# Two decoder layers on one core: gated loads of w_down, sums on VectorE, and four smaller moves in the order of work

## The chip, the core and the metric

The kernel runs on one core of a Trainium2 chip. The metric is the device time of one execution in microseconds (us), lower is better. It is given as the median of several runs. The profile comes from one more execution, whose own time is given beside its span.

The core has a matrix engine (TensorE, PE in the profile; PEld is its loading of weights), a vector engine (VectorE, DVE), a scalar engine (ScalarE, ACT), GpSimd (POOL), and SyncE (SP), which here only starts DMA transfers. Each engine works through its own queue in order; semaphores tie the queues together. Matmul results go to PSUM, everything else of the work lies in SBUF.

## The reference

Input and output are 512 tokens of 1024 channels in float32. Two layers of this form run one after the other, and an RMS norm closes:

```python
h = rmsnorm(x, norm_mix)
proj = h @ w_in                       # q, k, v of FoX, forget logits, q and kv of NSA, gates
log_f = log_sigmoid(f_a + b_forget)
y_a = fox_attention(q_a, k_a, v_a, log_f) @ w_o_fox    # scores carry c_i - c_j, c = cumsum(log_f)
y_b = nsa_attention(q_b, kv_b, g_b) @ w_o_nsa          # compressed, selected and window branch
x = x + (sigmoid(gate_a) * y_a + sigmoid(gate_b) * y_b) @ w_out
h = rmsnorm(x, norm_mlp)
x = x + square(relu(h @ w_up)) @ w_down                # w_up 1024 x 4096, w_down 4096 x 1024
```

Both attentions have 8 heads of 64. The forget logits need log_sigmoid and a running sum over the tokens.

## The kernel before

**Precision.** float32 operands are split into a rounded part h ("hi") and a rest ("lo"): ACT casts h, and VectorE (in a few places POOL) subtracts it to get the rest. A product is three matmuls, hi·hi, hi·lo and lo·hi, which is why pairs of a cast and a subtraction appear everywhere (L217/L218 for weights, L1255/L1256 for w_down's operands, L1618/L1619 for the activations).

**Stages of a layer.** Token projections of the values and of a group g2 (NSA values, forget logits, branch gates) come first. Then, in this order in the code: the casts of g2's values into VN together with the logits z and the tanh of the gates (L883 to L892), the gates, and forget() (L785 to L810), a chain of about twenty small VectorE operations with one Exp on ACT, whose result L801 feeds the matmuls L807/L808 into PSUM bank "S" (the running sum). Then fox_proj(0), the 8 FoX heads with other projections as filling, and the NSA heads in 4 pairs with more filling. A pair ends in after() (L962 on): ACT copies one half of PSUM to a tile "tmp" (L972), VectorE adds the other half (L973), twice, and out_pair (L497/L498) makes hi and lo. Both halves of a pair share one "tmp" tile.

Once all four pairs are there, half(1, m) for m = 0 to 7 multiplies them with w_o_nsa (gemm, L243 to L245; four k-tiles, one per pair, three matmuls each), gates the result and adds it to the FoX part. mix() splits it again, and w_out follows.

**mlp().** w_up's 32 columns of 128 activations: 8 are plain, the other 24 are made in units g = 4 to 15 by a Strassen–Winograd scheme of 2 × 2 blocks, with seven products instead of eight. w_down's last columns are units g = 16 to 19 of the same scheme. Unit g has two weight rows r1 = (a11, a12) and r2 = (s1, a22), and a third tile s3. SP loads them (L1456, L1466), and sums that the scheme needs are made by DMAs that POOL issues and that add while they write ("accumulating"):

- L1458: s1 in r2's first half; L1467: s3 from s3 and a11
- L1259: a11 becomes a11 + s1 (this is s2), once a11 itself has been cast
- L1261: a12 becomes a12 + s2 (this is s4)

operands(n) (L1244) casts the next n operands of w_down in the order of plan() and issues L1259 or L1261 behind the cast concerned. The products of w_down are L1302. Its moving operands are the activations as they are ("o", "ohl") and combinations of them: combine(p) (L1264) makes for each of the four groups p a tile "tf" with three VectorE operations (L1269, and L1271 twice) out of c[p], the two activations of one w_up unit, then its hi by ACT (L1273) and lo by VectorE (L1274) into a tile "tt". The results are added into x by VectorE (L1318 to L1336).

load(g) (L1438) takes the tiles of unit g out of pools and issues its loads. For g = 18 the tiles are one "vn" tile for r2 and r1, and half a "q2" tile for s3; g = 19 takes two more "q2" tiles and the other half. A load can start as soon as its tile's last user is done.

act() (L1607) finishes a w_up output: relu and square on ACT (L1616, L1617), hi on ACT (L1618), lo on POOL (L1619). 32 such activations are made; the last ones, which unit g = 15 makes, go to tiles "ohl".

**Order.** The work is written as generators that are advanced by hand. The order on each engine then follows from a scheduler; POOL's queue holds both its own arithmetic and the accumulating DMAs, and SP's queue holds all loads, those of the next layer behind those of w_down.

Of the kernel before, what the change touches and what calls it, by code (L numbers as in the profile page):

```python
# [11 lines left out]
F32 = mybir.dt.float32  # L12
F32R = mybir.dt.float32r
AF = mybir.ActivationFunctionType
OP = mybir.AluOpType
# [4 lines left out]
T = 512  # L20
KT = D // 128
NB = T // 128
# [10 lines left out]
OFF, N_SMALL = {}, 0  # L33
# [104 lines left out]
def run(*gens):  # L138
    for g in gens:
        for _ in g:  # L140
            pass


class Body:
# [471 lines left out]
    def compress(self, kc, vc, small, l):  # L616
# [20 lines left out]
        def load(c):  # L637
            for i, raw in enumerate(self.two("o2", "w1", F32) if c < 8 else ()):
                nc.sync.dma_start(raw, a["w1"][l, i, c].rearrange("p j m -> p (j m)"))
                loaded.append(raw)  # L640

        load(0)
        load(1)
        for c in range(0, 8, 2):
            load(c + 2)
# [205 lines left out]
    def layer(self, l, u):  # L851
        nc, a = self.nc, self.a
# [10 lines left out]
        R, rc = self.rstd(self.acc, ("O", "O"), wait=g, R=self.R)  # L863
        self.rc, self.late = rc, l > 0
        run(g)
        small = self.small
        g2 = [self.p(t) for t in ("mm", "mm", "O", "O")]
        g = self.token_proj([[a["wg2"][l, c].rearrange("p j m -> p (j m)")] for c in range(4)], 288, g2, u)
        VF = []
        for b in range(NB):  # L870
# [4 lines left out]
                                           op0=OP.mult, op1=OP.subtract)  # L875
# [2 lines left out]
        VN = self.t("vn", [128, NB, 4, 128], F32R)  # L878
        z = self.t("z", [128, NB, 8])
        th = self.t("th", [128, NB, 24])  # L880
        rch = self.t("s4", [128, NB], name="rch")
        nc.vector.tensor_scalar(rch, rc, 0.5, None, op0=OP.mult)
        for b in range(NB):  # L883
            pv = g2[b][:, :256].rearrange("p (h d) -> p h d", h=4)
            r = rc[:, b:b + 1]
            nc.vector.scalar_tensor_tensor(z[:, b], g2[b][:, 256:264], r, small[:, OFF["bf"]:OFF["bf"] + 8],
                                           op0=OP.mult, op1=OP.add)
            nc.scalar.activation(th[:, b], g2[b][:, 264:288], AF.Tanh, scale=rch[:, b:b + 1])
            nc.scalar.activation(VN[:, b, :, :64], pv, AF.Copy, scale=r)
            nc.vector.scalar_tensor_tensor(VN[:, b, :, 64:], pv, r, VN[:, b, :, :64].bitcast(F32),  # L890
                                           op0=OP.mult, op1=OP.subtract)
# [6 lines left out]
        nc.sync.dma_start(self.CRS, a["rope"])  # L898
        for i in range(2):
            nc.gpsimd.tensor_tensor(self.CRS[:, i], self.CRS[:, i], R, op=OP.mult)  # L900
        self.forget(z.rearrange("p b h -> p (b h)"))

        st, hl = {}, []

# [52 lines left out]
        def nsa_pair(p):  # L957

            hk = p // 2
            O = [None]  # L960

            def after(O):  # L962
                for e in range(2):
                    for bank in range(2):
                        nc.tensor.matmul(O[:, bank, e], self.vz[:, hk, e],
                                         self.pc[hk][p % 2][:, bank * 256:(bank + 1) * 256], start=False, stop=e == 1)
                o = self.t("zz", [128, T], name="o")
                t = self.t("tmp", [128, T])
                half = lambda x: x.rearrange("p (b c) -> p b c", b=2)
                for e in range(2):  # L970
                    s, f = slice(64 * e, 64 * e + 64), slice(64 * (1 - e), 64 * (1 - e) + 64)
                    nc.scalar.copy(half(t[s]), O[f, :, e])  # L972
                    nc.vector.tensor_add(half(o[s]), O[s, :, e], half(t[s]))  # L973
                st["ob", p] = self.out_pair(o)

            ready = (lambda: ("qb", p) in st and "ks" in st and "kw" in st, lambda: hk in self.pc)

            def unit(br, e):
                return dict(br=br, e=e, p=p, hk=hk, O=O, after=after, ready=ready[br], kk=lambda: KK[hk],
                            q=lambda: st["qb", p][:, e], v=lambda b: VN[:, b, 2 * br + hk],  # L980
                            gate=lambda: gt[:, :, 1 + br, 2 * p + e],
                            steps=(self.pair_scores, self.pair_transposes, self.pair_values))
            u = [unit(br, e) for br in range(2) for e in range(2)]
            for i in range(4):
                u[i]["other"], u[i]["second"] = u[(i + 2) % 4], u[i | 1]
            return u

        def half(kind, m, w):

            xs = ya if kind == 0 else yb  # L990
            ps = self.p("mm")
            yield from self.gemm(ps, w, 4 * (m % 2), xs, ks=4)
            st["y"] = ps
# [32 lines left out]
        yb = [st["ob", p] for p in range(4)]  # L1026
# [4 lines left out]
        def mix():  # L1031
            y = MA[len(mixed) // 2][:, len(mixed) % 2]
            h, lo = self.two("o2", "o")
            nc.scalar.activation(h, y, AF.Copy, scale=0.5)
            nc.vector.scalar_tensor_tensor(lo, y, 0.5, h.bitcast(F32), op0=OP.mult, op1=OP.subtract)
            mixed.append((h, lo))

        for m in range(8):
            if m % 2 == 0:
                w = self.weights(a["wo"][l, 1, m // 2].rearrange("p i c -> p (i c)"))  # L1040
            run(half(1, m, w))
            t, y = st["gb", m], MA[m // 2][:, m % 2]
            nc.vector.scalar_tensor_tensor(t, t, 1.0, st["y"], op0=OP.add, op1=OP.mult)
            nc.vector.tensor_add(y, y, t)
            if m % 2:
                mix()
# [9 lines left out]
        for m in range(8):  # L1056
            ps = self.bank()
            w = self.weights(a["wout"][l, m].rearrange("p k c -> p (k c)"))
# [11 lines left out]
    def mlp(self, l, x, u, acc, gm):  # L1070
# [35 lines left out]
        for j in range(self.PLAIN):  # L1106
            ps = self.bank()
            w = self.weights(a["wup"][l, j].rearrange("p k c -> p (k c)"))
            run(self.gemm(ps, w, 0, u))
            if R is None and j == 0:  # L1110
                pend.append(ps)
                continue
            if R is None:
                R, _ = self.rstd(acc, (self.turn_tag(), self.turn_tag()))
                prep = S.prepare(R)
                for p in pend:
                    act(p)
            act(ps)
            for _ in range(3):
                next(prep, None)  # L1120
# [89 lines left out]
class Strassen:  # L1210
# [33 lines left out]
    def operands(self, n):  # L1244

        b, nc = self.b, self.nc
        plan = self.plan()
        for k, g in plan[self.made:self.made + n]:
            self.made += 1
            r1, r2, s3 = self.raw[g]  # L1250

            a11, a12, s1 = r1[:, :512], r1[:, 512:], r2[:, :512]
            src = dict(a11=a11, a12=a12, s2=a11, s4=a12, s1=s1, a22=r2[:, 512:], s3=s3)
            h, lo = b.two("u2", "d")
            nc.scalar.copy(h, src[k])  # L1255
            nc.vector.tensor_tensor(lo, src[k], h.bitcast(F32), op=OP.subtract)  # L1256
            self.ops[k, g] = h, lo
            if k == "a11":
                nc.gpsimd.dma_start(a11, s1, accum_op=OP.add)  # L1259
            if k == "s2":  # L1260
                nc.gpsimd.dma_start(a12, a11, accum_op=OP.add)  # L1261
            yield
# [175 lines left out]
    def load(self, g, third=True):  # L1438

        b = self.b  # L1440
        if g == 18:
            r = b.t("vn", [128, 2, 1024], name="raw")
            r2, r1 = r[:, 0], r[:, 1]
            self.both = b.t("q2", [128, 2, 512], name="raw")
            s3 = self.both[:, 0]
        elif g == 19:
            r2, r1 = (b.t("q2", [128, 1024], name="raw") for _ in range(2))
            s3 = self.both[:, 1]
        elif g % 2:
            r2, r1, s3 = (b.t("va", [128, 1024], name="raw") for _ in range(3))  # L1450
        else:
            r2, r1 = (b.t("e", [128, 1536], name="raw") for _ in range(2))
            s3 = r1[:, 1024:]
        r1, r2, s3 = self.raw[g] = r1[:, :1024], r2[:, :1024], s3[:, :512]
        for i, t in enumerate((r2, r1)):
            self.nc.sync.dma_start(t, self.source(g, i))  # L1456
            if t is r2:
                self.nc.gpsimd.dma_start(r2[:, :512], r2[:, 512:], accum_op=OP.add)  # L1458
        if third:
            self.third(g)  # L1460
# [146 lines left out]
    def act(self, c, acts, tag):  # L1607

        b, nc = self.b, self.nc
        if tag == "kd":  # L1610
            if len(acts) % 2 == 0:
                self.late = b.t("kd" if len(acts) == 30 else "a4", [128, 4, T], F32R, name="ohl")
            h, lo = (self.late[:, len(acts) % 2 * 2 + i] for i in range(2))
        else:
            h, lo = b.two(tag, "o")
        nc.scalar.activation(c, c, AF.Relu)  # L1616
        nc.scalar.activation(c, c, AF.Square)  # L1617
        nc.scalar.copy(h, c)  # L1618
        nc.gpsimd.tensor_tensor(lo, c, h.bitcast(F32), op=OP.subtract)  # L1619
        acts.append((h, lo))  # L1620


# [34 lines left out]
```

## Time and profile before

| what | value |
|---|---|
| median of 3 runs | 1542.08 us (1542.0 to 1542.48) |
| the profiled execution's own time | 1543.98 us |
| its span | 1541.9 us |
| mean granted TensorE clock | 0.994 |
| PE, PEld busy | 1506.9 us, 1274.8 us |
| DVE, ACT, POOL busy | 1149.8 us, 835.3 us, 214.0 us |
| DMA | 199.35 MB, mean 129 GB/s |

A group or a piece of a timeline is read as: start, duration, engine, line, operation, output <- input, shape, count. In square brackets stands how long the engine was idle before it, and what ended that. A row of waits gives the engine, its tile and line, what it waited for, the total in us, the number of times and the longest. The granted clock is the share of full speed that the chip let TensorE have. A row of a table by stretches gives the stretch, its length, the busy time of each engine with the number of instructions, the granted clock, the DMA share and GB/s.

### The profile page before, as it was taken

What the parts mean: (1) busy time and instruction counts of PE and PEld (TensorE: products, weight loads), DVE (VectorE), ACT (ScalarE), POOL (GpSimd) and SP (SyncE); (2) the same over time, 40 slices, a digit from 0 to 9 for tenths busy, and PEclk for the clock granted to TensorE, in tenths of its full rate; (3) what the DMA queues carried; (4) which work ended last, traced back from release to release, by engine and by line L of the source; (5) the groups of instructions that cost most, each with busy time, mean ns of one, the idle gap of its engine ahead of it and who ended that gap; (6) DMA issues with size and microseconds to landing.
All of it is one profiled execution on the core that took longest, in us unless ns stands there. A gap on an engine that the chain in (4) does not pass through costs nothing. (4 is left out here: it accounts for less than half of the span.)

```text
span 1541.9 us, 22037 instructions
## 1 busy us (share of the span) xinstructions
PE 1506.9 (98%) x7952; PEld 1274.8 (83%) x7952; DVE 1149.8 (75%) x2188; ACT 835.3 (54%) x1580; POOL 214.0 (14%) x222
## 2 busy tenths in 40 slices
PE   9999999999999999998999999999999999999987
PEld 8888888887888888887987788888788888888976
DVE  5678978767487877787746799787674968777865
ACT  6465655554463655555534556555544637555645
POOL 4010000001200222223220000000011002212233
PEclk9999999999999999999999999999999999999999
DMA  7555422137324555556266552222453245555361
GB/s 267 158 162 134 131 69 82 56 110 211 96 96 144 144 144 138 136 138 177 75 192 169 161 136 82 93 69 69 150 171 107 91 144 144 137 140 148 96 145 61
DMA packets 73340, 199.35 MB, mean 129 GB/s; under 512 B 9200, under 2 KB 10608, under 8 KB 73232
## 3 DMA queue, kind: packets, MB, share of 16 engines
q1 hardware_dynamic: 57824, 170.41, 35.9%
q0 software_dynamic: 11520, 20.98, 7.8%
q10 hardware_dynamic: 3888, 6.58, 1.2%
q8 instruction: 62, 1.02, 0.3%
q14 instruction: 46, 0.38, 0.1%
HBM read 149.62 MB, written 4.19 MB: 100 GB/s over the span
## 5 line engine op out<-in xcount | busy, mean ns | idle before, releaser
L217 ACT CAST wh<-raw 128x1024 fp32r<-128x1024 f32 (+2 forms) x177 | 181.8, 1027 | 236.8 <-PE ps_mm L244 69.8
L218 DVE TENSOR_TENSOR wl<-raw,wh 128x1024 fp32r<-128x1024 f32 (+2 forms) x177 | 212.4, 1200 | 41.3 <-ACT wh L217 40.8
L243 PE MATMUL ps_mm<-u,wh 128*128 128x512 f32 x512 | 204.9, 400 | 0.0
L245 PE MATMUL ps_mm<-u,wl 128*128 128x512 f32 x512 | 202.0, 394 | 0.0
L244 PE MATMUL ps_mm<-u,wh 128*128 128x512 f32 x512 | 201.7, 394 | 0.0
L1486 DVE TENSOR_TENSOR s<-raw,s 128x512 fp32r<-128x512 f32 x168 | 138.4, 836 | 54.6 <-ACT s L1485 53.6
L1458 POOL DMA_DIRECT2D raw<-raw x32 | 29.1, 910 | 746.5 <-DVE wl L218 268.0
L1485 ACT CAST s<-raw 128x512 fp32r<-128x512 f32 x168 | 102.6, 620 | 29.3 <-PE ps_PT L1507 5.0
L243 PE MATMUL ps_mm<-o,wh 128*128 128x512 f32 x284 | 112.2, 396 | 1.8 <-ACT o L497 1.8
L243 PEld LDWEIGHTS ps_mm<-u,wh 128*128 128x128 f32 x512 | 96.7, 189 | 19.2 <-DVE E L457 0.8
L245 PEld LDWEIGHTS ps_mm<-u,wl 128*128 128x128 f32 x512 | 96.2, 188 | 19.7
L245 PE MATMUL ps_mm<-o,wl 128*128 128x512 f32 x284 | 111.4, 392 | 0.0
L244 PE MATMUL ps_mm<-o,wh 128*128 128x512 f32 x284 | 111.2, 392 | 0.0
L244 PEld LDWEIGHTS ps_mm<-u,wh 128*128 128x128 f32 x512 | 96.4, 188 | 16.6
L585 ACT CAST pth<-ps_PT 128x384 fp32r<-128x384 f32 (+1 forms) x96 | 49.0, 513 | 66.0 <-PE ps_PT L581 65.8
L543 DVE CUSTOM_DVE_ANT_0 E<-ps_S,ct 128x384 f32<-128x384 f32 (+3 forms) x112 | 57.3, 514 | 31.2 <-PE ps_S L556 30.3
L544 ACT ACTIVATE E<-E,tiny 128x384 f32<-128x384 f32 (+3 forms) x112 | 65.6, 586 | 20.2 <-DVE tiny L543 19.8
L243 PE MATMUL ps_PT<-o,wh 128*128 128x512 f32 x156 | 62.5, 401 | 6.0 <-DVE z L1555 6.0
L586 DVE TENSOR_TENSOR ptl<-ps_PT,pth 128x384 fp32r<-128x384 f32 (+1 forms) x96 | 56.8, 599 | 13.7 <-ACT pth L585 12.3
L243 PEld LDWEIGHTS ps_mm<-o,wh 128*128 128x128 f32 x284 | 53.3, 188 | 13.1 <-ACT o L497 2.6
L245 PEld LDWEIGHTS ps_mm<-o,wl 128*128 128x128 f32 x284 | 53.4, 188 | 11.7
L244 PEld LDWEIGHTS ps_mm<-o,wh 128*128 128x128 f32 x284 | 53.4, 188 | 10.6 <-DVE o L498 0.9
(448 smaller groups left out, 3741.4 us busy)
## 6 DMA issues: line engine op xcount, KB each, us to landing
raw<-wb SPq DMA_DIRECT2D x64, 512.0 KB
raw<-wup SPq DMA_DIRECT2D x64, 512.0 KB
raw<-wd SPq DMA_DIRECT2D x48, 512.0 KB
raw<-raw POOLq DMA_DIRECT2D x80, 256.0 KB, 4.4
w<-w SPq DMA_DIRECT2D x32, 256.0 KB
kda<-hla SPq DMA_DIRECT2D x32, 256.0 KB
q2a<-hla SPq DMA_DIRECT2D x64, 128.0 KB
raw<-wo SPq DMA_DIRECT2D x16, 512.0 KB
```

The lines of the kernel that those rows point to most:

```text
L217: nc.scalar.copy(h[:, :n], raw[:, :n])
L218: nc.vector.tensor_tensor(lo[:, :n], raw[:, :n], h[:, :n].bitcast(F32), op=OP.subtract)
L243: mm(ps, h[:, c], xh, start=start and i == 0, stop=False)
L244: mm(ps, h[:, c], xl, start=False, stop=False)
L245: mm(ps, lo[:, c], xh, start=False, stop=stop and i == ks - 1)
L543: nc.vector.tensor_tensor_reduce(e, ps, self.mask[:, T - n:], -1.0, BIG, OP.add, OP.min, mx)
L544: nc.scalar.activation(e, e, AF.Exp, bias=mx, scale=-1.0, accum_out=un["sm"][:, i:i + 1])
L585: nc.scalar.copy(h[:, e, :n], ps[:, :n])
L586: nc.vector.tensor_sub(lo[:, e, :n], ps[:, :n], h[:, e, :n].bitcast(F32))
L1458: self.nc.gpsimd.dma_start(r2[:, :512], r2[:, 512:], accum_op=OP.add)
L1485: nc.scalar.copy(h, src)
L1486: nc.vector.tensor_tensor(lo, src, h.bitcast(F32), op=OP.subtract)
```

## The change

There are six edits (line numbers of before):

1. The logits z and forget() are issued ahead of the casts of VN and the tanh of the gates (L878 to L901).
2. In a pair's after(), each half takes its own "tmp" tile (L968).
3. The last pair of heads is taken late: m = 0 and m = 1 of half(1, m) run over k-tiles 0 to 2 first, m = 0 into bank "mm" and m = 1 into bank "S", and then both take k-tile 3 (L1038 on).
4. a11 + s1 is made by VectorE, in the step that casts s2, and no longer by POOL's accumulating DMA L1259.
5. load(18) takes all tiles of units 18 and 19 at once and has ACT copy one column of c[3], which unit 15 of w_up makes last, into each of the four. The loads of units 18 and 19 write these tiles and so wait for the copies. In the queue r1 of a unit now stands ahead of r2.
6. act() has the lo half of the last two activations, 30 and 31, subtracted by VectorE, no longer by POOL.

```diff
@@ token projections, L878 @@
+        for b in range(NB):
+            nc.vector.scalar_tensor_tensor(z[:, b], g2[b][:, 256:264], rc[:, b:b + 1], small[:, OFF["bf"]:OFF["bf"] + 8],
+                                           op0=OP.mult, op1=OP.add)
+        self.forget(z.rearrange("p b h -> p (b h)"))
         rch = self.t("s4", [128, NB], name="rch")
...
-            nc.vector.scalar_tensor_tensor(z[:, b], g2[b][:, 256:264], r, small[:, OFF["bf"]:OFF["bf"] + 8],
-                                           op0=OP.mult, op1=OP.add)
...
-        self.forget(z.rearrange("p b h -> p (b h)"))
@@ after() of a pair, L965 @@
-                t = self.t("tmp", [128, T])
...
                     s, f = slice(64 * e, 64 * e + 64), slice(64 * (1 - e), 64 * (1 - e) + 64)
+                    t = self.t("tmp", [128, T])
@@ w_o_nsa, L1038 @@
-            run(half(1, m, w))
+            if m == 0:
+
+                first = [self.p(tag) for tag in ("mm", "S")]
+                for k, ks in ((0, 3), (3, 1)):
+                    for i, ps in enumerate(first):
+                        run(self.gemm(ps, w, 4 * i + k, yb[k:], ks=ks, start=k == 0, stop=k == 3))
+            if m < 2:
+                st["y"] = first[m]
+            else:
+                run(half(1, m, w))
@@ operands(), L1251 @@
+            if k == "s2":
+                nc.vector.tensor_tensor(a11, s1, a11, op=OP.add)
             h, lo = b.two("u2", "d")
             nc.scalar.copy(h, src[k])
             nc.vector.tensor_tensor(lo, src[k], h.bitcast(F32), op=OP.subtract)
             self.ops[k, g] = h, lo
-            if k == "a11":
-                nc.gpsimd.dma_start(a11, s1, accum_op=OP.add)
             if k == "s2":
                 nc.gpsimd.dma_start(a12, a11, accum_op=OP.add)
@@ load(), L1440 @@
         if g == 18:
             r = b.t("vn", [128, 2, 1024], name="raw")
+            self.rest = [b.t("q2", [128, 2, 512], name="raw") for _ in range(3)]
+
+            for t in [r] + self.rest:
+                self.nc.scalar.copy(t[:, :, :1], self.c[3][:, :, :1])
             r2, r1 = r[:, 0], r[:, 1]
-            self.both = b.t("q2", [128, 2, 512], name="raw")
-            s3 = self.both[:, 0]
+            s3 = self.rest[0][:, 0]
         elif g == 19:
-            r2, r1 = (b.t("q2", [128, 1024], name="raw") for _ in range(2))
-            s3 = self.both[:, 1]
+            r2, r1 = (t.rearrange("p a c -> p (a c)") for t in self.rest[1:])
+            s3 = self.rest[0][:, 1]
@@ act(), L1619 @@
-        nc.gpsimd.tensor_tensor(lo, c, h.bitcast(F32), op=OP.subtract)
+        (nc.vector if len(acts) > 29 else nc.gpsimd).tensor_tensor(lo, c, h.bitcast(F32), op=OP.subtract)
```

## The prediction, on record before the changed kernel ran

> **What bounds the kernel now.** First the page: is there an engine that is never idle?
>
> ```profile
> span 1541.9 us, 22037 instructions
> PE 1506.9 (98%) x7952; PEld 1274.8 (83%) x7952; DVE 1149.8 (75%) x2188; ACT 835.3 (54%) x1580; POOL 214.0 (14%) x222
> ```
>
> TensorE (PE) is. An edit can only pay where it closes a hole in PE's row, lets PE run at a higher clock, or shortens the few microseconds at both ends. No edit here removes a matmul. So the second view is the list of PE's waits, by what ended them (the columns behind the names: total, times, longest, in us).
>
> ```profile
> PE ps_PT L243 <- DVE z L1555: 6.0, 1, 6.0
> PE ps_mm L243 <- ACT o L497: 1.8, 2, 0.9
> PE ps_S L808 <- issue: 1.6, 1, 1.6
> PE ps_S L1302 <- DVE x L1328: 1.5, 1, 1.5
> ...
> PE ps_PT L1302 <- DVE x L1318: 1.5, 1, 1.5
> PE ps_PT L1302 <- ACT tt L1273: 1.4, 1, 1.4
> ...
> PE ps_PT L1302 <- POOL ohl L1619: 1.2, 1, 1.2
> ...
> PE ps_PT L1302 <- ACT ohl L1618: 1.1, 1, 1.1
> PE ps_S L808 <- DVE tiny L801: 1.0, 1, 1.0
> ...
> PE ps_mm L1302 <- POOL ohl L1619: 0.9, 1, 0.9
> ...
> PE ps_PT L1302 <- DVE tt L1274: 0.6, 1, 0.6
> ...
> PE ps_O L1302 <- DVE x L1318: 0.4, 1, 0.4
> ```
>
> Each row belongs to one place: 6.0 and L1328's 1.5 to w_down of layer 1, the seven others of L1302 (7.1 in all) to w_down of layer 0, 1.8 to the last pair of heads (one wait in each layer), L808's 1.6 and 1.0 to forget() of layers 0 and 1.
>
> Third, what ended the 6.0. ACT's, POOL's and SP's rows around it, then line 1259 (landing least, median, longest):
>
> ```profile
> 1467.06 0.62 ACT L1255 CAST d<-raw 128x512 fp32r<-128x512 f32 x1
> 1475.19 0.62 ACT L1255 CAST d<-raw 128x512 fp32r<-128x512 f32 x1 [7.50 <-DMA raw<-raw]
> ```
> ```profile
> 1468.32 1.14 POOL L1259 DMA_DIRECT2D raw<-raw  x1
> ```
> ```profile
> 1470.68 9.61 SPq L1456 DMA_DIRECT2D raw<-wdn  x3
> ```
> ```profile
> DMA to landing us min/median/max: 3.3/3.7/7.9
> ```
>
> ACT's cast of s2 needs the sum that line 1259 has a DMA make. That DMA was issued at 1468.32 and released ACT at 1475.19: 6.9 us, against a median of 3.7, while SP's loads of w_down ran over it. VectorE's queue stood behind ACT, and PE behind VectorE. Layer 0 shows the same (the 7.9).
>
> Fourth, the clock and the traffic there (span, then PE, PEld, DVE, ACT, POOL busy, granted clock, DMA share, GB/s):
>
> ```profile
> 715.00:727.00 12.00, 7.20 (x50) 6.04 (x48) 11.29 (x15) 8.88 (x14) 7.50 (x7) 1.00 0.95 232
> 727.00:730.00 3.00, 2.70 (x12) 2.70 (x13) 3.00 (x7) 0.00 (x0) 0.00 (x0) 0.50 0.18 71
> ...
> 734.00:737.00 3.00, 3.00 (x15) 3.00 (x15) 2.53 (x5) 1.66 (x3) 0.00 (x0) 0.50 0.00 0
> ...
> 1470.00:1477.00 7.00, 1.03 (x9) 0.82 (x8) 1.15 (x3) 1.81 (x4) 0.88 (x1) 0.82 1.05 297
> 1477.00:1480.00 3.00, 3.00 (x7) 2.40 (x8) 2.25 (x3) 2.97 (x6) 1.89 (x3) 0.50 0.60 128
> 1480.00:1483.00 3.00, 3.00 (x12) 2.35 (x11) 2.23 (x3) 1.17 (x3) 2.83 (x4) 0.78 0.69 143
> ```
>
> In layer 1, 0.82, 0.50 and 0.78 make 2.5 + 3.0 + 1.3 = 6.8 us at half clock; 2.5 lie before 1477, in the hole, so 4.3 us of work lose half: 2.1 us. A piece of half clock seems to last 3.4 us, and layer 0 has one about 727 and one about 734.
>
> **The change part by part.** The order of the changed kernel's instructions on each engine is known from its build; I walk through it with durations of before.
>
> *Layer 0, w_down: sums on VectorE (edit 4), lo halves on VectorE (edit 6), loads late (edit 5).*
>
> ```profile
> 715.66 0.69 DVE L1256 TENSOR_TENSOR d<-raw,d 128x512 fp32r<-128x512 f32 x1 [7.62 <-ACT d L1255]
> ...
> 720.56 1.75 DVE L1269 TENSOR_TENSOR tf<-z 128x512 f32<-128x512 f32 x1
> ```
> ```profile
> 733.68 0.74 PE L1302 MATMUL ps_PT<-tt,d 128*128 128x256 f32 x2 [0.64 <-DVE tt L1274]
> ```
>
> The sum needs no DMA any more, so VectorE's 7.62 us of idleness go. Two lo subtractions come in at 0.69 each, less about 1.1 where an operation lay beside POOL's subtraction (1.75 for what takes 0.69 alone). That is 7.3; the walk through the queue gives 7.0: the lo half of the fourth operand tile, which PE took at 733.68, is ready at 726.65. PE itself would be there at about 723.8 (733.68 less the 7.1 of waits, less 7 × 0.16 that a wait costs beside its own length, worked out at the last pair, and less 1.7 of half clock), so it waits anew, some 2.9 us. The gain is set by VectorE's chain: 7.0, plus 1.7 for the half-clock piece after 734 (the one at 727 lies ahead of that wait and costs nothing), less 1.0 for the chance that the new wait brings a piece of its own (0.6 of 1.7), less 0.2 for the new wait's own 0.16: **7.5**. From below 4.6 (two sums, 2 × 0.69, the gate copies, 0.8, and the rest of a half-clock piece, 0.7, all land on the chain), from above 9.9 (no wait left: 7.1 + 1.1 + 1.7).
>
> *Layer 1, w_down.* The 6.0 and the 2.1 of half clock go for the same reason: without them PE would reach the fourth operand tile, which it took at 1494.14, at about 1486.1. But edit 5 puts a wait in that place. The loads of pair 18 wait for gate copies behind the last cast of the activations on ACT; and VectorE's sum of pair 18 stands in its queue **ahead of** the last half of the tile's differences (L1271) and of the tile's lo half. Behind it queue those and every later addition into x; PE waits for them.
>
> ```profile
> 1480.58 0.62 ACT L1618 CAST ohl<-z 128x512 fp32r<-128x512 f32 x1
> ...
> 1492.95 1.05 ACT L1273 CAST tt<-tf 128x1024 fp32r<-128x1024 f32 x1 [1.84 <-DVE tf L1271]
> ```
> ```profile
> 1492.04 0.88 DVE L1271 SCALAR_TENSOR_TENSOR tf<-tf,z 128x256 f32<-128x256 f32 x2
> ```
> ```profile
> 1494.14 0.30 PE L1302 MATMUL ps_mm<-tt,d 128*128 128x256 f32 x1
> ```
> ```profile
> raw<-wdn SPq DMA_DIRECT2D x16, 512.0 KB
> ```
> ```profile
> DMA to landing us min/median/max: 3.3/4.7/11.2
> ```
> ```profile
> DMA to landing us min/median/max: 3.3/3.7/6.7
> ```
>
> (The last two are lines 1458 and 1467, the accumulations that make s1 and s3.) The cast that ended at 1481.2 ends some 5.8 earlier, 1475.4. The gates follow, and SP issues at 1475.7. At the 297 GB/s above, 512 KB take 1.76 us and 256 KB 0.88; the least landing, 3.3 for 256 KB, leaves 2.4 ahead of the data. So r1 is there at 1479.9, r2 at 1481.6, s3's load at 1482.5. With the medians s1 is summed at 1486.3 and s3 at 1486.2. Then 0.69 sum, 0.44 difference, 1.05 cast: the hi half is ready at 1488.5, PE waits about 2.5, and it stands where before stood at 1494.14: 5.5 gained. Then L1328's 1.5 goes: its chain of waits led to a DMA sum too, which VectorE now makes:
>
> ```profile
> 1496.66 4.46 DMA raw<-raw
> ```
>
> Less 0.6 for a chance of one in three that the new wait costs a piece of half clock: **6.4**. The ends: at the least landing (s3 then last, 1485.8) 6.9, with no half clock 7.5; at the longest (1492.8) the tile is ready at 1495.0, and the 5.5 turns into a loss of 0.9.
>
> *Last pair (edits 2, 3), both layers.*
>
> ```profile
> 352.06 0.58 ACT L972 COPY tmp<-ps_O 64x512 f32<-64x512 f32 x1 [0.75 <-DVE o L973]
> ```
> ```profile
> 352.58 0.39 PE L244 MATMUL ps_mm<-o,wh 128*128 128x512 f32 x1
> 352.81 0.39 PE L245 MATMUL ps_mm<-o,wl 128*128 128x512 f32 x1
> ```
>
> Matmuls start 0.23 apart. Five more of them, of m=1, now stand ahead of the first that needs the last pair: 1.16 us of cover against waits of 0.9. With its own tmp per half, ACT's second copy needn't wait the 0.75. Both waits go, and with each 0.16 more, because a matmul lasts 0.39 by its row and the next starts after 0.23 where nothing stops it: **2.1**. If the pair came later instead, the second PSUM bank would be the cause; ends 0 and 2.1. Elsewhere the split delays one pair by some 0.8 us, for which nobody waits.
>
> *forget() (edit 1).*
>
> ```profile
> 814.57 0.19 DVE L801 SCALAR_TENSOR_TENSOR tiny<-tiny 128x32 f32<-128x32 f32 x1
> ```
>
> L801 comes some 0.95 earlier, but its matmuls also stand five matmuls (1.16) earlier on PE, so the wait stays: **−0.3** for both layers, ends −2.3 and +1.9.
>
> *At nothing:* four gate copies per layer (0.2 each, ACT is busy 54%; they lie behind the last cast, counted above); the next layer's weights, which stand behind the gated loads on SP and are used only after this stage; if they ran late, each us would cost the next layer one.
>
> Sum: 7.5 + 6.4 + 2.1 − 0.3 = 15.7. The profiled execution took 1543.98, 2.1 more than its span and 1.9 more than the median, 1542.08. So 1528.3 on the former, **1526.4** on the latter.
>
> **The rivals.**
>
> *A. The gated loads give layer 1 back* (0.17). For it: VectorE's sum stands ahead of the tile, and landings of 11.2 occur. Against: few other loads are then under way. At 11.2 layer 1 loses 0.9 rather than gains 6.4: 1542.1 − 7.5 − 2.1 + 0.3 + 0.9 = 1533.7; so 1529.5 to 1534.
>
> *B. No new wait* (0.12). The pair lands while PE is still on older tiles, and the lists of VectorE drain faster than I walk: 9.9 + 6.1 + 2.1 + 1.7 + 2.1 − 0.3 = 21.6 gained: 1520.5; 1519.5 to 1523.
>
> *C. The new waits without half clock* (0.17). The row 727 to 730 has 0.50 although no single wait ahead of it is above 1.5 us; that bears out that short waits in a row suffice, and I have charged 1.6 for it. If they don't: 1524.8. The Trainium skill, “TensorE: Matmul & The Clock Gate”, section “HAM oscillation — how this bites in real kernels”, asks only that no idle gap exceed about 3.4 us; by that rule the new waits, each shorter, would be free, and the outcome is C. This trace speaks against the rule as far as its row at 727 goes.
>
> *D. Slower* (0.06). The same place as A, further: if s1 of pair 18 lands past 1501.2, the tile comes 9.3 us later than in before and eats the rest (7.5 + 2.1 − 0.3); at 1505.1 the time is 1546. It would need 23.5 us from issue to landing, twice the longest here.
>
> *E. Within 0.2%* (0.06): VectorE, at 11.29 of 12 us busy in layer 0, doesn't get its extra sums done (8 × 0.69) and loses there what layer 1 gains: some 1541.
>
> **How the numbers follow.** The forecast has 0.42 (1524.5 to 1529.5). The range of 8 in 10 takes in C, A and the upper half of B: 1521.5 to 1534. A measurement of this kernel tells about 0.2%, 3.1 us, from no change. Faster by more: 0.42 + 0.17 + 0.12 + 0.17 = 0.88; within: 0.06; slower: 0.06.
>
> **What would show it.** PE's waits on L1555, L497, L1318 and POOL's lo are gone; a wait on tt of 2 to 3 us stands in each w_down; VectorE's sum of pair 18 in layer 1 waits for a DMA until about 1486; L808's waits remain. Wrong if the holes of before stay, if that sum waits beyond 1490, or if PE's clock falls for more than one piece per layer.

## The result, and the profile after

The changed kernel takes 1523.56 us (median of 4 runs, 1521.22 to 1525.26), before 1542.04 (4 runs, 1541.21 to 1542.48). The ratio is 0.988, 95% interval 0.9863 to 0.9897: 18.5 us faster. The forecast was 1526.4, in a range of 1521.5 to 1534, and a gain of 15.7 us. The profiled execution took 1524.42, 19.6 less than that of before.

The head of the page, and the rows of PE's waits that answer to those of before (the line numbers have moved: L1302 is now L1312, tt's L1273 and L1274 are L1283 and L1284):

```profile
span 1522.6 us, 22041 instructions
...
PE 1500.2 (99%) x7952; PEld 1271.8 (84%) x7952; DVE 1147.7 (75%) x2200; ACT 836.0 (55%) x1588; POOL 201.5 (13%) x210
```
```profile
PE ps_mm L1312 <- ACT tt L1283: 2.8, 1, 2.8
PE ps_PT L1312 <- ACT tt L1283: 1.6, 1, 1.6
...
PE ps_S L808 <- DVE tiny L801: 0.8, 1, 0.8
...
PE ps_PT L1312 <- DVE tt L1284: 0.6, 1, 0.6
...
PE ps_S L808 <- issue: 0.4, 1, 0.4
```

The 6.0 behind VectorE's z, the 1.8 of the last pairs, POOL's lo halves, and the waits on x L1318, L1324 and L1328 are gone. What stands in w_down now, up to the last stage of layer 1, are waits for the fourth operand tile tt: 1.6 and 0.6 in layer 0, 2.8 in layer 1.

Both traces have 7952 matmuls, so the start of the n-th in each (counted from 0) tells how far ahead the changed kernel is, and the step between two such points what a stage gave:

| matmul n | before | after | ahead | step | stage between |
|---|---|---|---|---|---|
| 200 | 38.97 | 38.55 | 0.4 | 0.4 | start of the program |
| 1000 | 191.38 | 189.84 | 1.5 | 1.1 | forget() of layer 0 |
| 1600 | 308.68 | 306.92 | 1.8 | 0.2 | |
| 2000 | 393.52 | 390.41 | 3.1 | 1.3 | last pair, layer 0 |
| 3500 | 694.53 | 691.55 | 3.0 | −0.1 | |
| 3950 | 764.57 | 753.25 | 11.3 | 8.3 | w_down, layer 0 |
| 4500 | 866.59 | 854.98 | 11.6 | 0.3 | forget() of layer 1 |
| 5600 | 1079.31 | 1067.43 | 11.9 | 0.3 | |
| 5900 | 1143.30 | 1130.09 | 13.2 | 1.3 | last pair, layer 1 |
| 7400 | 1449.33 | 1435.87 | 13.5 | 0.2 | |
| 7940 | 1532.46 | 1513.16 | 19.3 | 5.8 | w_down, layer 1, and the end |

Now the new wait in layer 1. First the chain that ended last, in order of time, in the stretch that leads to it (start, length, what); then VectorE's row of the sum of pair 18; then ACT's gate copies:

```profile
1462.28 4.71 DMA raw<-wdn
...
1467.03 4.90 DMA raw<-raw
1471.93 1.42 issue
1473.34 0.69 DVE raw L1265
1474.04 0.34 DVE tf L1281
...
1474.40 1.05 ACT tt L1283
...
1475.50 0.58 PE ps_mm L1312
```
```profile
1473.34 0.69 DVE L1265 TENSOR_TENSOR raw<-raw 128x512 f32<-128x512 f32 x1 [2.91 <-issue]
```
```profile
1461.17 0.47 ACT L1456 COPY raw<-z 128x2 f32<-128x2 f32 x4
```

Gates, a load, an accumulating DMA, VectorE's sum, the last difference, the cast, and PE: these are the links that were foreseen. VectorE stood idle for 2.91 us at the sum, with the tile's last difference behind it in the queue. The DMA of the chain is the one that makes s1 (L1471). The 1.42 behind it, which the chain calls issue, ends as another lands, the one that makes s3 out of a11 (L1480; POOL's row, and the time from issue to landing):

```profile
1467.66 1.14 POOL L1480 DMA_DIRECT2D raw<-raw  x1
```
```profile
DMA to landing us min/median/max: 5.6/5.6/5.6
```

That is until 1473.3. It reads a11, which the sum overwrites, so the sum most likely waited for both; the profile names no releaser. The prediction had reckoned with both, at 1486.3 and 1486.2.

The stretches around both new waits (columns as before; the granted clock is the third figure from the end):

```profile
720.00:723.50 3.50, 1.21 (x8) 0.91 (x8) 1.75 (x3) 1.04 (x1) 1.35 (x2) 1.00 1.13 211
723.50:727.50 4.00, 3.96 (x22) 3.76 (x21) 2.98 (x6) 2.28 (x4) 0.00 (x0) 0.59 0.47 83
...
1472.50:1475.50 3.00, 0.17 (x3) 0.00 (x1) 1.38 (x4) 1.10 (x2) 1.43 (x2) 0.94 0.94 164
1475.50:1478.50 3.00, 3.00 (x14) 3.00 (x15) 1.81 (x2) 0.47 (x1) 0.03 (x1) 0.50 0.53 93
```

Behind each wait lies a piece of half clock: 0.41 × 4.0 / 0.5 = 3.3 us of layer 0's stretch, and 0.50 throughout the 3.0 us of layer 1's.

### The profile page after: what moved, and what is told of

Same layout as the page of the kernel before. It is cut to its first block, busy times and chain, and to the rows that moved or that the text cites. A ratio compares the mean times of both kernels' runs of the same rounds, so it can differ in the third digit from the quotient of the medians.

```text
span 1522.6 us, 22041 instructions
## 1 busy us (share of the span) xinstructions
PE 1500.2 (99%) x7952; PEld 1271.8 (84%) x7952; DVE 1147.7 (75%) x2200; ACT 836.0 (55%) x1588; POOL 201.5 (13%) x210
## 4 chain that ended last, share of the span: by engine, by line
PE 86%; DVE 6%; ACT 4%; issue 2%; DMA 1%; POOL 0%; DVEq 0%; SPq 0%; ACTq 0%; POOLq 0%
PE ps_mm L243 11%; PE ps_mm L245 11%; PE ps_mm L244 11%; PE ps_PT L243 3%; PE ps_PT L245 3%; PE ps_PT L244 3%; PE ps_O L1520 3%; PE ps_S L1520 3%; PE ps_O L607 2%; PE ps_PT L581 2%; PE ps_S L556 2%; PE ps_PT L1520 2%; PE ps_mm L1520 2%; PE ps_S L243 2%; PE ps_S L245 2%
## 5 line engine op out<-in xcount | busy, mean ns | idle before, releaser
L1471 POOL DMA_DIRECT2D raw<-raw x32 | 28.2, 882 | 770.5 <-PE ps_PT L581 239.5
L243 PE MATMUL ps_mm<-o,wh 128*128 128x512 f32 x276 | 109.2, 396 | 0.0
L245 PE MATMUL ps_mm<-o,wl 128*128 128x512 f32 x276 | 108.3, 392 | 0.0
L244 PE MATMUL ps_mm<-o,wh 128*128 128x512 f32 x276 | 108.0, 391 | 0.0
L243 PE MATMUL ps_PT<-o,wh 128*128 128x512 f32 x156 | 61.4, 394 | 0.0
L245 PE MATMUL ps_PT<-o,wl 128*128 128x512 f32 x156 | 61.0, 391 | 0.0
L244 PE MATMUL ps_PT<-o,wh 128*128 128x512 f32 x156 | 60.9, 390 | 0.0
```

Of the source, the lines that this page charges most:

```text
L243: mm(ps, h[:, c], xh, start=start and i == 0, stop=False)
L244: mm(ps, h[:, c], xl, start=False, stop=False)
L245: mm(ps, lo[:, c], xh, start=False, stop=stop and i == ks - 1)
```

## The experiments

Theory 1: the holes of before were made by the accumulating DMA of line 1259 in the chain ACT, VectorE, PE; taking it out (edit 4) is enough, and the gates (edit 5) only cost. Theory 2: the collision with the loads of pairs 18 and 19 made them, and the gates are what helps. Times are medians in us; the ratio is to the kernel before on the same chip.

| kernel | median | ratio, 95% interval |
|---|---|---|
| the changed kernel | 1523.6 | 0.988 (0.9863 to 0.9897) |
| edit 4 alone | 1525.0 | 0.9884 (0.9867 to 0.9901) |
| edit 5 alone | 1541.0 | 0.9987 (0.9973 to 1.0) |
| edits 3 and 4 alone | 1522.0 | 0.9872 (0.9857 to 0.9887) |
| changed, without 5 | 1518.2 | 0.9839 (0.9821 to 0.9858) |
| changed, gates on c[2] | 1520.2 | 0.9857 (0.9838 to 0.9875) |
| changed, sums of 18 and 19 by DMA | 1527.5 | 0.9902 (0.9885 to 0.992) |
| changed, without 6 | 1525.9 | 0.9896 (0.9883 to 0.991) |
| changed, without 3 | 1526.6 | 0.9901 (0.9887 to 0.9914) |
| changed, without 1 | 1523.7 | 0.9879 (0.9865 to 0.9892) |
| without 5, fourth tile in pieces | 1516.5 | 0.9837 (0.9824 to 0.9851) |
| without 5 and 6, in pieces | 1519.9 | 0.9857 (0.9843 to 0.9872) |

### Edit 4 alone

```diff
 (before)
+            if k == "s2":
+                nc.vector.tensor_tensor(a11, s1, a11, op=OP.add)
             h, lo = b.two("u2", "d")
...
-            if k == "a11":
-                nc.gpsimd.dma_start(a11, s1, accum_op=OP.add)
```

> The kernel before with edit 4 alone: a11 + s1 by VectorE, loads ungated, everything else as before. Theory 1 (the DMA in the chain): the holes in w_down come from ACT's cast of s2 waiting for an accumulating DMA, and it is enough to take that DMA out of the chain, whatever the loads do. Then the wait on L1555 in layer 1 (6.0), its half clock (2.1) and the 1.5 on L1328 go, and layer 0 gains about 5 to 7 although its lo halves stay on POOL: 1526 to 1530. Theory 2 (the collision): the early loads of pairs 18 and 19 are the cause; they would now slow the accumulations of s1 and s3, VectorE's sum would wait for these instead: 1535 to 1541.

1525.0: theory 1, a little below its range. Of PE's waits in w_down up to the final stage only the fourth tile's are left:

```profile
PE ps_PT L1302 <- ACT tt L1273: 2.4, 1, 2.4
PE ps_mm L243 <- ACT o L497: 1.8, 2, 0.9
...
PE ps_mm L1302 <- ACT tt L1273: 1.5, 1, 1.5
```

No wait on POOL's lo halves is in the list, though POOL still makes them. In before POOL's queue had stood still until the sum of L1259 landed, which L1261 adds on, and the lo halves of layer 0 came behind it:

```profile
715.57 0.87 POOL L1261 DMA_DIRECT2D raw<-raw  x1 [7.39 <-DMA raw<-raw]
```

So those waits came of the same hole. The time can't be told from that of the whole change.

### Edit 5 alone

```diff
 (before)
+            self.rest = [b.t("q2", [128, 2, 512], name="raw") for _ in range(3)]
+
+            for t in [r] + self.rest:
+                self.nc.scalar.copy(t[:, :, :1], self.c[3][:, :, :1])
...
```

> The kernel before with edit 5 alone: loads of pairs 18 and 19 gated, a11 + s1 still by an accumulating DMA. Theory 1: the DMA lands in its usual 3.3 to 3.7 us instead of 6.9 and 7.9, so some 3.5 to 4.5 us per layer go and the rest of the wait stays; late loads may cost up to 3 in layer 1: 1533 to 1538. Theory 2: with no collision both holes close entirely: 1526 to 1529.

1541.0: neither theory foresaw so little. Line 1259 (least, median, longest landing), ACT's row at the cast of s2, and PE's waits:

```profile
DMA to landing us min/median/max: 3.3/3.5/4.9
```
```profile
1466.76 0.62 ACT L1255 CAST d<-raw 128x512 fp32r<-128x512 f32 x1 [5.59 <-DMA raw<-raw]
```
```profile
PE ps_S L1302 <- DVE x L1328: 4.4, 1, 4.4
PE ps_PT L243 <- DVE z L1558: 4.1, 1, 4.1
PE ps_PT L1302 <- ACT tt L1273: 2.5, 1, 2.5
```

The longest landing fell from 7.9 to 4.9, so the loads did lengthen it; but the hole of layer 1 went only from 6.0 to 4.1, because the DMA still stands in the chain. And the late loads opened another of 4.4 at the DMA sum of pair 19, where before had 1.5. Theory 2 falls.

### The changed kernel without edit 5

```diff
 (changed)
-            for t in [r] + self.rest:
-                self.nc.scalar.copy(t[:, :, :1], self.c[3][:, :, :1])
...
```
(with the tiles of load(18) and load(19) allocated as in before)

> The changed kernel without edit 5: loads of pairs 18 and 19 start as soon as their tiles are free, as before. Theory 1: the gates bring nothing once VectorE makes the sum; the loads start about 6 us earlier, VectorE's sum of pair 18 in layer 1 finds its data, and the wait of 2.8 us on the fourth operand tile goes with the 1.7 of half clock behind it: 1518.5 to 1520.5. Theory 2: the early loads slow the accumulations for pair 17 again and holes come back: 1527 or more.

1518.2, a little below theory 1's range and 5.4 less than with the gates, and the intervals of the ratios don't meet. Its waits on the tile:

```profile
PE ps_PT L1312 <- ACT tt L1283: 1.8, 1, 1.8
...
PE ps_PT L1312 <- DVE tt L1284: 0.6, 1, 0.6
```

Both lie in layer 0; the 2.8 of layer 1 is gone, though the sum of pair 18 stands at the same place in VectorE's queue. So theory 1 holds, and the wait was the lateness of the gated loads.

### Gates on an earlier output

```diff
 (changed)
-                self.nc.scalar.copy(t[:, :, :1], self.c[3][:, :, :1])
+                self.nc.scalar.copy(t[:, :, :1], self.c[2][:, :, :1])
```

> The changed kernel with the gates on c[2] (unit 14's output) in place of c[3]: the loads of pairs 18 and 19 start some 3 to 4 us earlier than in the changed kernel, later than without gates. If the wait of 2.8 us in layer 1 is the lateness of these loads, it shrinks with their start, to between 0 and 1, and the half-clock piece behind it goes: 1518 to 1521. If only their collision matters, nothing changes or it gets longer: 1523 or more.

1520.2. VectorE comes to the sum without any idle time before it, and layer 1 has no wait on the tile and no half clock there:

```profile
1471.47 0.69 DVE L1265 TENSOR_TENSOR raw<-raw 128x512 f32<-128x512 f32 x1
```

As expected of late loads.

### Sums of pairs 18 and 19 given back to POOL's DMA

```diff
 (changed)
-            if k == "s2":
+            if k == "s2" and g < 18:
                 nc.vector.tensor_tensor(a11, s1, a11, op=OP.add)
...
+            if k == "a11" and g > 17:
+                nc.gpsimd.dma_start(a11, s1, accum_op=OP.add)
```

> The changed kernel with the sums of pairs 18 and 19 given back to POOL's accumulating DMA; VectorE sums pairs 16 and 17 only. VectorE's queue then has no wait for the gated loads ahead of the last differences of the fourth tile. If that wait makes the 2.8 us hole of layer 1: the hole and its half clock (1.7) go, 1518.5 to 1520.5, and PE's first matmul of that tile comes without a wait. If VectorE's own work is what makes the tile late, it stays at 1522 to 1525. If the DMA sum comes too late for pair 18 itself, ACT waits for it and PE gets a new hole on s2 of 18: 1524 or more.

1527.5, the third case: the wait on the tile in layer 1 is gone, and in its place stand two waits of PE for additions behind the casts of s2. VectorE's idle time in that stretch:

```profile
1478.25 0.69 DVE L1268 TENSOR_TENSOR d<-raw,d 128x512 fp32r<-128x512 f32 x1 [3.83 <-ACT d L1267]
...
1483.79 0.69 DVE L1268 TENSOR_TENSOR d<-raw,d 128x512 fp32r<-128x512 f32 x1 [4.51 <-ACT d L1267]
```

These two cost 2.5 and 3.6 on PE, and the granted clock is 0.50 from 1480.55 to 1490.79. With late loads, one more DMA in the chain is worse than VectorE standing idle.

### Without edit 6

```diff
 (changed)
-        (nc.vector if len(acts) > 29 else nc.gpsimd).tensor_tensor(lo, c, h.bitcast(F32), op=OP.subtract)
+        nc.gpsimd.tensor_tensor(lo, c, h.bitcast(F32), op=OP.subtract)
```

> The changed kernel without edit 6: the lo halves of activations 30 and 31 by POOL again. Theory 1 (with the sum's DMA out of the chain these lo halves are early enough, and VectorE's freed 1.4 us pays for the stretching beside POOL): 1522 to 1525 and no wait of PE on POOL. Theory 2 (POOL's lo is late by itself): PE waits in layer 0 for POOL's lo, 1.2 and 0.9 as in before, 1525 to 1528.

1525.9; the interval overlaps that of the changed kernel, and the profiled execution is 3.8 us longer in its span (1526.4 against 1522.6). PE waits for POOL's lo nowhere, against theory 2; the loss lies in layer 1, where VectorE's queue waits for both gated sums:

```profile
1473.93 0.69 DVE L1265 TENSOR_TENSOR raw<-raw 128x512 f32<-128x512 f32 x1 [2.80 <-DMA raw<-raw]
...
1481.83 0.69 DVE L1265 TENSOR_TENSOR raw<-raw 128x512 f32<-128x512 f32 x1 [3.49 <-DMA raw<-raw]
```

POOL's accumulation ahead of the second was issued at 1475.89, against 1472.24 in the changed kernel. In POOL's queue the accumulation L1271 of pair 18 (1475.26) stands ahead of it there, and behind it in the changed kernel. So neither theory as worded: in these two profiles edit 6 pays by the order of VectorE's and POOL's queues at the gates; that it pays in the time is not certain.

### Without edit 3, with edit 2

```diff
 (changed)
-            if m == 0:
-
-                first = [self.p(tag) for tag in ("mm", "S")]
...
+            run(half(1, m, w))
```

> The changed kernel without edit 3, edit 2 kept: half(1, 0) runs over all four pairs at once again, each half of a pair keeps its own tmp. If the second copy's wait of 0.75 on the shared tmp was real, the chain is that much shorter and the two waits on L497 come back as about 0.2 each: 1523.5 to 1524.5. If the split of tmp brings nothing, the waits come back with 0.9 each and what lay beside them (1.4 per layer by the count of matmuls): 1525.5 to 1527.

1526.6, the second case. The waits are those of before to a tenth:

```profile
PE ps_mm L243 <- ACT o L497: 1.8, 2, 0.9
```

And in the changed kernel itself ACT's second copy, now with a tmp of its own, still waits for VectorE's addition:

```profile
350.29 0.58 ACT L973 COPY tmp<-ps_O 64x512 f32<-64x512 f32 x1 [0.75 <-DVE o L974]
```

Edit 2 shortens nothing; why the copy still waits is not shown. Edit 3 brings it all, 1.3 per layer.

### Without edit 1

```diff
 (changed)
-        self.forget(z.rearrange("p b h -> p (b h)"))
         rch = self.t("s4", [128, NB], name="rch")
...
+        self.forget(z.rearrange("p b h -> p (b h)"))
```
(and the logits z back inside the loop)

> The changed kernel without edit 1: z and forget() behind the casts of VN again. Count of matmuls in the two profiles: the edit brought 1.2 us in layer 0 and 0.2 in layer 1. If so 1524.5 to 1526, with waits on L808 of 1.6 and 1.0. By the prediction (no gain, minus 0.3) 1522.5 to 1523.8.

1523.7, the same as with the edit: the expected 1524.5 to 1526 and the waits of 1.6 and 1.0 did not come, the waits are 0.6 and 0.8. These waits scatter: over the five profiles with the old place (before, edit 4, edit 5, edits 3 and 4, this one) both layers together waited 2.6, 1.9, 2.0, 1.9 and 1.4; over the eight with the new place between 0.2 and 1.8, 0.8 in the mean. That makes some 1.1 for edit 1, too little for a single comparison of times to show.

### Edits 3 and 4 alone

> The kernel before with edits 3 and 4 alone: sums of w_down's operands on VectorE, last pair of heads taken late; no gates, lo halves on POOL, forget() and tmp as before. By the runs so far edit 4 alone is 1525.0 and edit 3 is worth 1.4 per layer: 1521.5 to 1523, so two edits do what the whole change does (1523.6). If edit 3 needs edit 2's second tmp, its waits come back: 1524 to 1525.5.

1522.0 (the diff is those of edits 4 and 3 on the kernel before). Two of the six edits do what the six do. The wait on L497 is gone without edit 2.

### The fourth tile in pieces, without the gates

```diff
 (changed, without edit 5)
-        self.nc.scalar.copy(o[:, :, 0], t)
-        V.tensor_tensor(o[:, :, 1], t, o[:, :, 0].bitcast(F32), op=OP.subtract)
+        for s in (slice(1, 2), slice(2, 4), slice(0, 1)) if p == 3 else (slice(0, 4),):
+            self.nc.scalar.copy(o[:, s, 0], t[:, s])
+            V.tensor_tensor(o[:, s, 1], t[:, s], o[:, s, 0].bitcast(F32), op=OP.subtract)
```

> The changed kernel without edit 5, and in combine() the fourth tile's hi and lo are made in three pieces, the one that s2 needs first. If VectorE's chain on this tile makes layer 0's remaining wait (1.8 and 0.6 without the gates), the hi half comes some 0.7 earlier and the lo half some 1.5 earlier: the waits shrink to about 1, and if the half-clock piece behind them goes as well, 1515 to 1516.5; with that piece, 1516.5 to 1518. If PE waits for something else there: 1518 to 1519.5.

1516.5, the lowest of all; against 1518.2 the intervals overlap, so the times alone don't separate the two. The profiles do: the waits in layer 0 are 0.6 and 0.6 rather than 1.8 and 0.6, and the clock behind them stays full.

```profile
PE ps_PT L1313 <- DVE x L1335: 0.6, 1, 0.6
PE ps_PT L1313 <- ACT tt L1284: 0.6, 1, 0.6
```
```profile
719.00:722.00 3.00, 1.76 (x13) 1.35 (x12) 2.58 (x7) 2.58 (x6) 0.00 (x0) 1.00 0.35 64
722.00:726.00 4.00, 4.00 (x34) 4.00 (x35) 3.90 (x9) 1.63 (x3) 0.00 (x0) 1.00 0.00 0
```

So VectorE's chain on this tile did make layer 0's wait.

### The same, without edit 6

> The changed kernel without edit 5 and with the fourth tile in pieces (1516.5), and without edit 6 as well: lo halves of activations 30 and 31 by POOL. With the gates, giving up edit 6 brought new waits of 2.8 and 1.6 in layer 1. If those came from POOL's queue being late with the gated accumulations behind its own subtractions, they don't come here: 1515.5 to 1517.5. If POOL's subtraction is late by itself, 1518 to 1520.

1519.9 (the diff is that of edit 6 above): the time is in the second case's range. No wait on gated sums comes, but PE waits 1.1 and 0.7 for the tile in layer 1, and 0.9 and 0.7 in layer 0. Without gates, too, edit 6 seems worth keeping; the intervals overlap, so the 3 us between the medians are not certain.

## Why the prediction was right, and where its terms were off

**Layer 0, w_down: 7.5 forecast, 8.3 found.** The mechanism is as foreseen: no wait for the sum, VectorE back to back, a new wait for the fourth tile. Its lo half was to be ready at 726.65, counted in the time of before; PE took it at 723.01 and the changed kernel was 3.0 ahead there, so 726.0. The new wait was to be 2.9 and is 1.6 + 0.6 = 2.2. The half-clock piece, charged with 1.0, came in full (1.7). At matmul 3792 (744.59 before, 734.05 after) the changed kernel was 10.5 ahead, so the terms named make 7.5. The other 0.8 is a wait of before later in the stage, at 755, which the prediction's list left out:

```profile
PE ps_mm L1302 <- DVE x L1324: 0.8, 1, 0.8
```


**Layer 1, w_down: 6.4 forecast, 5.8 found.** The sum of pair 18 was to wait until 1486.3; it came at 1473.34 + 13.5 = 1486.8. The hi half was to be ready at 1488.5; it was at 1475.4 + 13.5 = 1488.9. The new wait was to be 2.5 and is 2.8, and at the tile (matmul 7673) the lead is 18.8: 5.3 gained, 5.5 forecast. The term that was too small is the half clock, charged with 0.6 at one in three. The piece came, and by matmul 7727 the lead is 17.5: it cost 1.3, since its first 0.38 us lay in the wait. L1328's wait went, as forecast, and gave 1.8 rather than 1.5.

**Last pair: 2.1 forecast, 2.7 found,** by one of the two causes given. The five matmuls of m = 1 cover the wait, also without edit 2; the step by which the second tmp saves ACT's 0.75 failed.

**forget(): −0.3 forecast, 1.1 + 0.3 found in the two profiles,** and some 1.1 by all profiles together. The sign was wrong. VectorE's last step L801, in before (layer 0) and in the changed kernel (both layers):

```profile
53.89 0.19 DVE L801 SCALAR_TENSOR_TENSOR tiny<-tiny 128x32 f32<-128x32 f32 x1
```
```profile
51.15 0.18 DVE L801 SCALAR_TENSOR_TENSOR tiny<-tiny 128x32 f32<-128x32 f32 x1
...
802.30 0.18 DVE L801 SCALAR_TENSOR_TENSOR tiny<-tiny 128x32 f32<-128x32 f32 x1
```

In layer 0 it came 2.7 earlier, 0.4 of which the kernel was ahead anyway: 2.3 rather than the 0.95 of the forecast, and that is the mis-sized term; what made the difference was not traced. In layer 1 it came 12.3 earlier, with 11.3 to 11.6 of lead: 0.7 to 1.0, as forecast.

**The total.** The profiles differ by 19.3 us of span, 3.6 more than the sum forecast. The four terms make 2.5 of that (0.8 − 0.6 + 0.6 + 1.7). The rest lies in stages for which no term was given, 0.4 of it before forget(), and is not explained. So part of the nearness is luck: an uncounted wait, a wrong sign and a layer 1 that gave less than forecast lie within it.

**What the sum couldn't see.** The prediction weighed edits 4 and 5 as one remedy, since both bear on the same collision. They are not: edit 4 alone gives 17.8 by its median (1542.8 to 1525.0), edit 5 alone 1.8 with an interval that reaches no change, and edit 5 on top of the others costs 5.4. The cost was in the sum (the new wait of layer 1); that nothing stood against it was not. Rival A had this place and this mechanism, but a larger price than it took; and by the prediction's own walk the loss of 0.9 replaces only the 5.5 and not all 6.4, so its time would have been 1532.8 and not 1533.7. Rival D would have needed a landing of 23.5 us; the chain shows 4.90. Rivals B and E didn't come.

**Rival C fell,** though in layer 0 by little: in the changed kernel the clock gave way behind waits of 2.8 us, and of 1.6 and 0.6 close together, but without edit 3 the same 1.6 and 0.6 left it full (see the last section). The Trainium skill, “TensorE: Matmul & The Clock Gate”, section “HAM oscillation — how this bites in real kernels”, sets the limit at an idle gap of about 3.4 us; by this trace's 2.83 with a clock of 0.50 behind it, that is too lenient here.

## What to carry to other kernels

When a transfer is slow because another runs over it, ask first whether it must stand in the chain at all: an engine's own 0.69 us took the place of 3.3 to 7.9 us of DMA, and made the remedy for the collision superfluous, even harmful. Measure edits that aim at the same stall one at a time: here one of two gave all, and the other took 5 us back. When an engine waits for data in a strict queue, what counts is what stands behind it; a tile that PE needs next should not.

## What was not expected of the hardware

Half clock for about 3.4 us follows waits much shorter than that, and not at a fixed length: a single wait of 2.8 drew it (the changed kernel, layer 1), waits of 1.8 and 0.6 within 3 us drew it (without edit 5, layer 0), and so did a single one of 1.8 (without edit 6, layer 0); a single one of 2.3 did not in the kernel with edits 3 and 4 alone, while one of 2.4 did in that with edit 4 alone.

The kept traces show what decides. Wherever one has several pieces of half clock, they start a whole number of times 3.413 us apart: those of the changed kernel at 724.18 and 1475.12, and 750.9 is 220 × 3.413. So each execution can be cut into slots of that length. In the changed kernel both waits of layer 0 fall into one slot, in which PE is busy for 1.75 of 3.41 us, and the next slot has half clock. Without edit 3 the same two waits lie across the border of two slots, with 2.08 and 2.50 busy, and the clock stays full:

```profile
720.77:724.18 3.41, 1.75 (x10) 1.35 (x11) 1.85 (x3) 1.55 (x3) 0.89 (x1) 1.00 1.11 201
724.18:727.59 3.41, 3.41 (x17) 3.41 (x18) 2.41 (x6) 1.65 (x3) 0.00 (x0) 0.50 0.34 59
```
```profile
718.59:722.00 3.41, 2.08 (x18) 1.87 (x16) 2.38 (x5) 0.88 (x1) 0.86 (x1) 1.00 1.07 323
722.00:725.41 3.41, 2.50 (x16) 2.10 (x17) 2.62 (x5) 1.56 (x4) 0.89 (x1) 1.00 1.08 193
725.41:728.80 3.39, 3.39 (x31) 3.39 (x30) 3.29 (x7) 1.52 (x3) 0.00 (x0) 1.00 0.16 27
```

The 2.3 and the 2.4 are told apart in the same way: the 2.3 lies across a border (first two rows), the 2.4 in one slot:

```profile
716.14:719.55 3.41, 2.48 (x21) 2.27 (x19) 3.41 (x8) 1.34 (x3) 0.89 (x1) 1.00 0.79 140
719.55:722.96 3.41, 2.04 (x15) 1.85 (x15) 3.38 (x5) 1.04 (x1) 0.00 (x0) 1.00 0.11 19
```
```profile
720.71:724.12 3.41, 1.05 (x9) 0.85 (x8) 3.41 (x8) 1.05 (x1) 0.00 (x0) 1.00 0.45 79
724.13:727.54 3.41, 3.41 (x18) 3.41 (x17) 2.04 (x5) 0.85 (x2) 0.00 (x0) 0.50 0.48 154
```

Over all thirteen profiles, the last 20 us of each left out, half clock began behind 18 slots, and PE was idle in them for 1.60 us or more; of all other slots at full clock one reached 1.62 and none else more than 1.56. In the last 20 us the two kinds overlap, between 1.1 and 1.7. No run shifted the slots on purpose. By these traces a wait of about 1.7 to 3 us costs up to 1.7 more if it falls into one slot, and nothing more if a border halves it; where the borders lie differs from profile to profile.
